# Encoder block on one core: the last stage's loads in program order on SP's queue at fixed steps, its first blocks fetched during the stage ahead, and its row sums one per step

## The chip, the core and the metric

The kernel runs on one core of a Trainium2 chip. The metric is the time of one execution in microseconds (us), taken on the device; lower is better. The profile is one further execution, recorded instruction by instruction. Engine names: PE is TensorE (matmul), PEld its weight loads, DVE is VectorE, ACT is ScalarE, POOL is GpSimd, SP is SyncE, which here only issues DMAs. Each engine works through its own list of instructions in order, and one that has to wait holds up those behind it on the same engine.

## The reference, cut to what matters

One encoder block on 1024 tokens of width 1024, in float32: a layer norm, one wide projection, dilated attention and a bidirectional recurrence, a merge with a second layer norm, then a gated feed-forward part with a third one. The change is in the feed-forward part:

```
gate, up = split(h @ w_ffn_in)                       # 1024 x 2816 each
h = layer_norm(ALPHA * h + (silu(gate) * up) @ w_ffn_out)   # w_ffn_out: 2816 x 1024
```

## The kernel before, in words

**Precision.** Every float32 operand is split into a high part `hi` (a cast, on ACT, line 204) and the rest `lo` (a subtraction, line 208, on POOL for weights, on DVE for activations here). `mm3` (lines 227 to 231) multiplies with three matmuls: hi by hi, one of hi and lo each way. Each writes one PSUM bank of 128x512.

**The two feed-forward stages.** `ffn_in` (line 1375) makes the 22 blocks of the activation, 128 rows by 1024 tokens each, and `ffn_out` (line 1480) multiplies them by `w_ffn_out`. Both use the seven products of a Strassen-Winograd scheme in place of eight. For `ffn_out` the activation is cut into a11, a12, a21, a22 (two halves of the 22 blocks, two halves of the tokens), the weights into b11, b12, b21, b22 (two halves of the rows, two halves of the columns). `combine` in `ffn_in` forms a11, a12, s2 (stored once, float32) and s1, s3, s4, a22 (stored already split, two tensors each) and writes them to scratch memory `gd` from SP's queue (lines 1408 and 1414). `ffn_in` ends with the last of its own seven products and `combine(10, 1)`.

**The work of `ffn_out`.** Six products run in the order 1, 2, 6, 5, 7, 3, each over 11 blocks j: 66 *steps*, numbered here from 0. A step multiplies one activation block by one weight block for four token tiles t: 12 matmuls, into four banks X (`pj`: products 1, 6, 7) or Z (`sd`: products 2, 5, 3). Product 4 follows, with the loops turned: for t = 0 to 3, 33 matmuls into X[t] over the a22 columns of that tile. After each of the six products its four banks are added to the halves of the row tiles Y[0] to Y[7] (`add`, line 1531: the "row sums", on DVE from PSUM). Product 4 gives the last sum of Y[4 + t].

**What a step needs.**

- the activation block: for products 1, 2, 6 a load `graw` (line 1504, three buffers), then `ghi` on ACT and `glo` on DVE (three buffers); for products 5, 7, 3 two loads straight into `ghi` and `glo` (line 1508);
- the weight block: 128x512 of `w_ffn_out` (`Wb11` and so on, line 1493; each has a buffer of its own), combined on DVE (`right`, lines 1511 to 1529: five subtractions or additions for each j), then split into `w_hi`, `w_lo` (four buffers).

Product 4 needs `a22h` and `a22l` of its tile (line 1597, 704 KB each, two buffers: tiles 2 and 3 reuse those of 0 and 1).

**The end.** `finish(t)` (line 1535) makes the layer norm of one row tile: two `bn_stats` and an aggregate on DVE, a power on POOL (line 198), the scaling on ACT (line 252), a product with the gain on POOL (line 1550), a sum on DVE (line 1551), and a store from SP's queue (line 1552). Tile 7 is done in halves, on DVE alone. The order in the code is t = 0 to 3 inside the loop over product 4's tiles, then 4 to 7.

**What sets the order.** The program is written in the order of the code, then a scheduler places each engine's instructions by its own estimate of when they can start; buffers add the waits. Instructions under `high_priority` (the row sums) are drawn forward. So SP's list of DMA issues need not follow the code.

Of the kernel before, what the change touches and what calls it, by code (L numbers as in the profile page):

```python
# [10 lines left out]
F32 = mybir.dt.float32  # L11
F32R = mybir.dt.float32r
# [7 lines left out]
D = 1024  # L20
T = 1024
KT = D // 128
HALF = 512
# [3 lines left out]
NJ = NF // 2  # L27
# [54 lines left out]
class Block:  # L82
# [1292 lines left out]
    def ffn_in(self):  # L1375

        nc = self.nc
        with ExitStack() as es:
# [99 lines left out]
    OUT_G = {1: "a11", 2: "a12", 6: "s2", 5: "s1", 7: "s3", 3: "s4"}  # L1478

    def ffn_out(self):  # L1480
# [3 lines left out]
        with ExitStack() as es:  # L1484
            wb = es.enter_context(self.pool("fow"))
            rp = es.enter_context(self.pool("for", "right"))
            W, Y = {}, {}
            halves = [slice(HALF * h, HALF * (h + 1)) for h in range(2)]

            def load(n, j):  # L1490
                W[n, j] = t = wb.tile([128, HALF], F32, name=f"W{n}", tag=f"{n}{j}", bufs=1)
                k, c = int(n[1]) - 1, int(n[2]) - 1
                nc.sync.dma_start(t, self.wfo[128 * (j + NJ * k):128 * (j + NJ * k + 1), HALF * c:HALF * (c + 1)])

            def rows(t):
                Y[t] = y = rp.tile([128, D], F32, name="y2", tag=f"y2{t}", bufs=1)
                nc.sync.dma_start(y, self.ahs_d[t])

            def acts(p, j):
                d = self.gd[self.OUT_G[p]][j]  # L1500
                z = [rp.tile([128, HALF], F32R, name=f"g{n}", tag=f"g{n}", bufs=3) for n in ("hi", "lo")]
                if len(d) == 1:
                    r = self.ws.tile([128, HALF], F32, name="graw", tag="wsum", bufs=3)
                    nc.sync.dma_start(r, d[0])
                    self.split(*z, r, eng_lo="dve")
                else:
                    for t, s in zip(z, d):
                        nc.sync.dma_start(t.bitcast(F32), s)
                return z

# [24 lines left out]
            def finish(t):  # L1535
                y = Y[t]
# [16 lines left out]

            for j in range(NJ):
                load("b11", j)
            X = [self.ps_pj(t) for t in range(4)]
            Z = [self.ps_sd() for t in range(4)]
            late = {}
            for p in self.OUT_ORDER:
                bank = X if p in (1, 6, 7) else Z  # L1560
                for j in range(NJ):
                    if p == 1:
                        load("b21", j)
                        if j in (3, 5, 7, 9):
                            rows((j - 3) // 2)
                    if p == 2:
                        load("b12", j)
                        if j >= NJ - 3:
                            load("b22", j - NJ + 3)
                    if p == 6 and j + 3 < NJ:  # L1570
                        load("b22", j + 3)
                    if p == 5 and j in (1, 3, 5, 7):
                        rows(4 + j // 2)
                    if p == 5 and j == 9:
                        g2, b2 = (rp.tile([128, D], F32, name=n) for n in ("g2", "b2"))
                        for t, v in zip((g2, b2), self.ln["2"]):
                            nc.scalar.dma_start(t, bass.AP(tensor=v.tensor, offset=v.offset, ap=[[0, 128], [1, D]]))
                    g = acts(p, j)
                    w = self.granules()
                    w = [z.rearrange("p k c -> p (k c)") for z in w]  # L1580
                    self.split(*w, right(p, j))
# [8 lines left out]
                for t in range(4):  # L1590
                    for i, h in {1: ((0, 0),), 2: ((0, 0),), 6: ((0, 1),), 5: ((1, 1),), 7: ((1, 1),), 3: ((0, 1),)}[p]:
                        add(4 * i + t, h, bank[t])
            a22 = []
            for t in range(4):
                a22.append([rp.tile([128, NJ, 128], F32R, name=f"a22{z}", tag=f"a22{z}", bufs=2) for z in "hl"])
                for z, d in zip(a22[t], self.gd["a22"]):
                    nc.sync.dma_start(z.bitcast(F32), d[:, :, 128 * t:128 * (t + 1)])  # L1597
            for t in range(4):
# [4 lines left out]
                finish(t)  # L1603
            for t in range(4, 8):
                finish(t)
# [38 lines left out]
```

## Time and profile before

| | |
|---|---|
| time, median of 3 runs | 2185.49 us (2185.03 to 2187.88) |
| the profiled execution's own time | 2187.32 us |
| its span in the profile, first to last instruction | 2185.5 us |
| PE busy in the span | 2037.5 us (93%) |
| DVE, ACT, POOL busy | 1380.8, 920.1, 1217.8 us |
| mean clock granted to PE | 0.979 of full |
| last matmul of `ffn_in` before the first of `ffn_out` | about 1920.5 us |
| PE's waits in `ffn_out`, up to 1986 us | 9.24, 1.87, 12.15 and 11.86 us |

In rows of the timeline the first number is the start in us from the span's beginning, the second the length; "x3" means that three like instructions are merged into a row; a bracket at the end says how long the engine sat idle before it and what it was released by. SPq rows are DMA issues. In the table by stretches (windows) the columns are the stretch, its length, busy time of PE, PEld, DVE, ACT, POOL with the number of instructions, the granted PE clock as a share of full, the busy share of the DMA engines and GB/s.

### The profile page before, as it was taken

The numbers are of one execution on the slowest core, as the hardware profiler recorded it, in microseconds if no ns is written. First come the engines' busy times: TensorE is split into PE (matmuls) and PEld (weight loads), VectorE is DVE, ScalarE is ACT, GpSimd is POOL, SyncE is SP. The second block draws the span as 40 slices with busy tenths as digits, with TensorE's granted clock in tenths as the row PEclk, the third lists the DMA queues.
The fourth block names the chain that finished last, engine by engine and source line by source line (L and its number), as shares of the span: only waits on it lengthen the run. The fifth ranks groups of instructions, "written<-read, shape, count | busy, mean of one in ns | idle before, by whom it ended". The sixth has DMA issues, their size and how long they took to land.

```text
span 2185.5 us, 31268 instructions
## 1 busy us (share of the span) xinstructions
PE 2037.5 (93%) x10941; PEld 1677.8 (77%) x10941; DVE 1380.8 (63%) x2165; ACT 920.1 (42%) x1870; POOL 1217.8 (56%) x960
## 2 busy tenths in 40 slices
PE   4799999999999999999999999998999999957997
PEld 3678887778877888778887788786888888846886
DVE  7667646875378845867455523258778878757426
ACT  6544455443554436344463421244434434323421
POOL 3566553566436664655545763444667777623545
PEclk9899999999999999999999999999999999988999
DMA  5343442435333352434436663335444445395454
GB/s 205 98 129 102 150 143 83 145 113 164 113 122 125 125 168 95 132 116 133 150 101 218 216 222 120 105 113 164 154 149 146 166 142 179 126 340 170 140 193 159
DMA packets 296447, 324.20 MB, mean 148 GB/s; under 512 B 15905, under 2 KB 212834, under 8 KB 296290
## 3 DMA queue, kind: packets, MB, share of 16 engines
q1 hardware_dynamic: 288544, 295.76, 42.1%
q10 hardware_dynamic: 7746, 26.45, 3.1%
q8 instruction: 86, 1.41, 0.3%
q14 instruction: 71, 0.58, 0.1%
HBM read 211.78 MB, written 110.36 MB: 147 GB/s over the span
## 4 chain that ended last, share of the span: by engine, by line
PE 59%; DVE 6%; POOL 4%; DMA 4%; issue 4%; ACT 1%; SPq 1%; DVEq 0%; POOLq 0%; ACTq 0%
PE pj L229 12%; PE pj L230 12%; PE pj L231 12%; PE sd L231 6%; PE sd L229 6%; PE sd L230 6%; POOL w_lo L208 2%; DMA Wb<-in_w_ffn_out_dram 1%; PE sd L1023 1%; DVE hR L984 1%; DVE hR L983 1%; DMA wa<-in_w_in_dram 1%; DMA graw<-ga11f 1%; DVE qd L938 0%; SPq L1597 0%
## 5 line engine op out<-in xcount | busy, mean ns | idle before, releaser
L208 POOL TENSOR_TENSOR w_lo<-wa,w_hi 128x512 fp32r<-128x512 f32 x276 | 387.0, 1410 | 273.6 <-ACT w_hi L204 265.7
L204 ACT CAST w_hi<-wa 128x512 fp32r<-128x512 f32 x276 | 170.0, 618 | 227.8 <-PE pj L230 164.4
L208 POOL TENSOR_TENSOR w_lo<-wsum,w_hi 128x512 fp32r<-128x512 f32 x88 | 135.7, 1553 | 78.3 <-ACT w_hi L204 40.9
L208 POOL TENSOR_TENSOR w_lo<-f_raw,w_hi 128x512 fp32r<-128x512 f32 x66 | 109.0, 1664 | 66.6 <-ACT w_hi L204 65.5
L208 POOL TENSOR_TENSOR w_lo<-Wb,w_hi 128x512 fp32r<-128x512 f32 x55 | 74.2, 1350 | 119.3 <-ACT w_hi L204 114.1
L229 PE MATMUL pj<-xt1hi,w_hi 128*128 128x512 f32 x268 | 109.2, 408 | 22.0 <-ACT xt1hi L204 15.7
L230 PE MATMUL pj<-xt1lo,w_hi 128*128 128x512 f32 x268 | 107.6, 402 | 4.5 <-DVE xt1lo L208 4.5
L231 PE MATMUL pj<-xb22hi,w_lo 128*128 128x512 f32 x268 | 105.1, 392 | 2.4 <-POOL w_lo L208 2.4
L231 PE MATMUL pj<-xt1hi,w_lo 128*128 128x512 f32 x268 | 106.8, 399 | 0.0
L229 PE MATMUL pj<-xb22hi,w_hi 128*128 128x512 f32 x268 | 105.7, 394 | 0.1
L463 POOL TENSOR_TENSOR wa<-wa,wa 128x512 f32<-128x512 f32 x46 | 64.5, 1403 | 73.5 <-DVE ws L462 65.5
L230 PE MATMUL pj<-xb22lo,w_hi 128*128 128x512 f32 x268 | 104.8, 391 | 0.0
L208 POOL TENSOR_TENSOR w_lo<-ws,w_hi 128x512 fp32r<-128x512 f32 x46 | 67.4, 1469 | 63.0 <-ACT w_hi L204 60.9
L229 PE MATMUL pj<-w_hi,ghi 128*128 128x512 f32 x132 | 55.1, 418 | 35.1 <-ACT ghi L204 35.1
L485 ACT COPY wkeep<-pj 128x512 f32<-128x512 f32 x138 | 80.3, 582 | 11.4 <-DVE evh L377 5.9
L229 PE MATMUL pj<-xb11hi,w_hi 128*128 128x512 f32 x188 | 77.5, 413 | 7.0 <-DVE wkeep L402 5.5
L204 ACT CAST w_hi<-wsum 128x512 fp32r<-128x512 f32 x88 | 54.6, 620 | 65.1 <-PE sd L230 61.7
L1393 ACT ACTIVATE fth<-fc 128x512 f32<-128x512 f32 x44 | 27.8, 632 | 122.3 <-DVE fc L1392 122.3
L229 PEld LDWEIGHTS pj<-xt1hi,w_hi 128*128 128x128 f32 x268 | 51.8, 194 | 35.8 <-ACT xt1hi L204 16.3
L388 DVE TENSOR_TENSOR evh<-wkeep,pj 128x512 f32<-128x512 f32 x48 | 32.7, 680 | 73.7 <-PE pj L231 53.7
L975 ACT ACTIVATE hS<-hR,dec 128x128 f32<-128x128 f32 x112 | 44.5, 402 | 80.9 <-DVE hR L984 57.6
L229 PE MATMUL pj<-xt4hi,w_hi 128*128 128x512 f32 x188 | 74.8, 398 | 3.6 <-DVE evh L377 3.6
(405 smaller groups left out, 6703.6 us busy)
## 6 DMA issues: line engine op xcount, KB each, us to landing
wa<-in_w_in_dram SPq DMA_DIRECT2D x184, 256.0 KB, 3.1
f_raw<-in_w_ffn_in_dram SPq DMA_DIRECT2D x44, 512.0 KB, 4.2
Wb<-in_w_ffn_out_dram SPq DMA_DIRECT2D x44, 256.0 KB, 5.4
tg<-evh SPq DMA_DIRECT2D x32, 256.0 KB, 3.0
tg<-tg SPq DMA_DIRECT2D x16, 512.0 KB, 3.9
y<-ahs SPq DMA_DIRECT2D x16, 512.0 KB, 6.1
ah<-xt ACTq DMA_DIRECT2D x8, 512.0 KB, 6.6
rec<-hg ACTq DMA_DIRECT2D x8, 512.0 KB, 4.0
```

The source lines that it names most:

```text
L204: nc.scalar.copy(hi, src)
L208: e.tensor_sub(lo, src, hi.bitcast(F32))
L229: nc.tensor.matmul(ps, whi, xhi, start=first, stop=False, **kw)
L230: nc.tensor.matmul(ps, whi, xlo, start=False, stop=False, **kw)
L231: nc.tensor.matmul(ps, wlo, xhi, start=False, stop=last, **kw)
L388: nc.vector.tensor_add(t, add, ps)
L463: nc.gpsimd.tensor_sub(a["a21"], a["a11"], a["a21"])
L485: nc.scalar.copy(t, ps)
L975: nc.scalar.activation(S[:, c, :], E, AF.Copy, scale=dec[:, 1, c:c + 1])
L983: nc.vector.scalar_tensor_tensor(En, E, dec[:, 1, c:c + 1], ps[:, jj, :], op0=OP.mult, op1=OP.add)
L984: nc.vector.tensor_scalar(En, En, dec[:, 0, c:c + 1], None, op0=OP.mult)
L1393: nc.scalar.activation(th[:, s], c[:, s], AF.Tanh, scale=0.5)
```

## The change: what it does

1. **Kept in order.** All loads of `ffn_out` go through `queued`, which issues them from SP's queue and has the scheduler keep them in the order in which the code gives them. The stores of the finished rows do not go through it. The two vectors of the layer norm, which ACT's queue loaded, come through it as well.
2. **Fixed steps.** A table (`bulk`) says at which step each load that is not the step's own activation block is issued, right behind that block: b11 from block 4 at steps 0 to 6, b21 at 7 + j, b12 at 16 + j, b22 at 17 + j, rows Y[0] to Y[3] at 11 to 14, Y[4] to Y[7] at 33, 35, 37, 39, the vectors at 46 and 48, a22 of tiles 0 and 1 at 55 to 61. The a22 loads of tiles 2 and 3 stand at the head of their own turn of the loop over product 4's tiles.
3. **First blocks ahead.** `out_begin`, called in `ffn_in` ahead of its last product, loads b11 blocks 0 to 3 into the buffers `w_raw` (idle by then) and the first three `graw`, and splits step 0.
4. **Row sums one per step.** The four sums of products 1, 6 and 7 are given one by one in the steps of the next product (from its fifth block on after product 1); those of 2, 5 and 3 still come together.
5. **Finishing.** Tile 4 + t is finished in turn t; turns 0 and 1 also finish tiles 0, 1 and 2, 3.

The diff, cut to its core:

```diff
+            self.out_begin()
             next(held, None)
             combine(NJ - 1, 1)
...
+    def queued(self, o, i):
+        return self.tc.keep_in_program_order(self.nc.sync.dma_start(o, i))
...
+    def out_begin(self):
+        self.W = W = {}
+        for i in range(2):
+            r = self.wraw.tile([128, D], F32, name="w_raw", tag="wraw", bufs=2)
+            for k in range(2):
+                W["b11", 2 * i + k] = self.out_block(r[:, HALF * k:HALF * (k + 1)], "b11", 2 * i + k)
+            if i == 0:
+                raw = self.out_raw(1, 0)
+                g, w = self.flat(), self.flat()
+                self.split(*w, W["b11", 0])
+                self.split(*g, raw, eng_lo="dve")
+        self.begun = {(1, 0): (g, w)}
+        self.raws = {(1, j): self.out_raw(1, j) for j in (1, 2)}
...
+            def last_acts(t, i):
+                if i == 0:
+                    a22.append([rp.tile([128, NJ, 128], F32R, name=f"a22{z}", tag=f"a22{z}", bufs=2) for z in "hl"])
+                self.queued(a22[t][i].bitcast(F32), self.gd["a22"][i][:, :, 128 * t:128 * (t + 1)])
...
+            for j in range(NJ):
+                at(7 + j, load, "b21", j)
+                at(16 + j, load, "b12", j)
+                at(17 + j, load, "b22", j)
+            for t in range(4):
+                at(11 + t, rows, t)
+                at(33 + 2 * t, rows, 4 + t)
...
+                    if adds and (p != 2 or j > 4):
+                        add(*adds.pop(0))
...
-            a22 = []
             for t in range(4):
-                a22.append([rp.tile([128, NJ, 128], F32R, name=f"a22{z}", tag=f"a22{z}", bufs=2) for z in "hl"])
-                for z, d in zip(a22[t], self.gd["a22"]):
-                    nc.sync.dma_start(z.bitcast(F32), d[:, :, 128 * t:128 * (t + 1)])
-            for t in range(4):
+                if t >= 2:
+                    for i in range(2):
+                        last_acts(t, i)
                 for j in range(NJ):
                     self.mm3(X[t], a22[t][0][:, j, :], a22[t][1][:, j, :], *late[j], False, j == NJ - 1,
                              skip_group_check=True)
                 add(4 + t, 0, X[t])
-                finish(t)
-            for t in range(4, 8):
-                finish(t)
+                if t < 2:
+                    finish(2 * t)
+                    finish(2 * t + 1)
+                finish(4 + t)
```

**Three places in the order of instructions.** Numbers behind names only tell buffers apart. First, SP's list before, where loads for product 1 (`graw` of a11, blocks 7 and 8) stand among the weights of the later products, the last rows (`y2`) and the a22 blocks; blocks 9 and 10 come behind all of these:

```order
L1504 DMA graw_17712<-ga11f7_209 128x512
L1493 DMA Wb22_18111<-in_w_ffn_out_dram 128x512
L1493 DMA Wb22_18138<-in_w_ffn_out_dram 128x512
L1493 DMA Wb22_18165<-in_w_ffn_out_dram 128x512
L1493 DMA Wb22_18192<-in_w_ffn_out_dram 128x512
L1493 DMA Wb22_18219<-in_w_ffn_out_dram 128x512
L1504 DMA graw_17736<-ga11f8_210 128x512
L1493 DMA Wb22_18246<-in_w_ffn_out_dram 128x512
L1493 DMA Wb22_18273<-in_w_ffn_out_dram 128x512
L1497 DMA y2_18400<-ahs4_119 128x1024
```

The same blocks of product 1 on SP's list with the change:

```order
L1484 DMA graw_17688<-ga11f7_209 128x512
L1484 DMA Wb21_17696<-in_w_ffn_out_dram 128x512
L1484 DMA graw_17712<-ga11f8_210 128x512
L1484 DMA Wb21_17720<-in_w_ffn_out_dram 128x512
L1484 DMA graw_17736<-ga11f9_211 128x512
L1484 DMA Wb21_17744<-in_w_ffn_out_dram 128x512
L1484 DMA graw_17760<-ga11f10_212 128x512
L1484 DMA Wb21_17768<-in_w_ffn_out_dram 128x512
L1484 DMA graw_17784<-ga12f0_213 128x512
```

One weight block now stands between two activation blocks; the rest of b21, b12, b22, the rows and a22 moved behind them.

Second, the end of SP's list before, from the last block of product 3 on (`y2_17608`, `17658`, `17708`, `17758` are Y[0] to Y[3], `y2_18400` is Y[4]):

```order
L1508 DMA glo_19112<-gs4l10_300 128x512
L1597 DMA a22h_19148<-ga22h_301 128x11x128
L1597 DMA a22l_19149<-ga22l_302 128x11x128
L1552 DMA out_0_dram<-y2_17608 128x1024
L1597 DMA a22h_19152<-ga22h_301 128x11x128
L1597 DMA a22l_19153<-ga22l_302 128x11x128
L1552 DMA out_0_dram<-y2_17658 128x1024
```

The same place with the change (`y2_17794`, `17820`, `17846`, `17872` are Y[0] to Y[3], `18382`, `18428`, `18474` are Y[4] to Y[6]):

```order
L1484 DMA glo_19118<-gs4l10_300 128x512
L1594 DMA out_0_dram<-y2_17794 128x1024
L1594 DMA out_0_dram<-y2_17820 128x1024
L1594 DMA out_0_dram<-y2_18382 128x1024
L1594 DMA out_0_dram<-y2_17846 128x1024
L1594 DMA out_0_dram<-y2_17872 128x1024
L1594 DMA out_0_dram<-y2_18428 128x1024
L1484 DMA a22h_19286<-ga22h_301 128x11x128
L1484 DMA a22l_19287<-ga22l_302 128x11x128
L1594 DMA out_0_dram<-y2_18474 128x1024
L1484 DMA a22h_19336<-ga22h_301 128x11x128
L1484 DMA a22l_19337<-ga22l_302 128x11x128
```

The a22 blocks of tile 2 moved from ahead of every store to behind six of them, the sixth that of Y[5]; those of tile 3 from behind Y[0]'s store to behind Y[6]'s.

Third, DVE's list between the `glo` of the first and of the second block of product 6. Before:

```order
L208 TENSOR_TENSOR glo_18087<-graw_18088,ghi_18086 128x512
L1520 TENSOR_TENSOR wt2_18202<-Wb22_18111,Wb11_17512 128x512
L208 TENSOR_TENSOR glo_18114<-graw_18115,ghi_18113 128x512
L1533 TENSOR_TENSOR y2_17608<-y2_17608,sd_17530 128x512
L1533 TENSOR_TENSOR y2_17658<-y2_17658,sd_17531 128x512
```

With the change:

```order
L208 TENSOR_TENSOR glo_18077<-graw_18078,ghi_18076 128x512
L1565 TENSOR_TENSOR Wb21_17844<-Wb21_17844,Wb11_17576 128x512
L1568 TENSOR_TENSOR Wb12_18091<-Wb22_18118,Wb12_18091 128x512
L1561 TENSOR_TENSOR Wb11_17600<-Wb12_18120,Wb11_17600 128x512
L1570 TENSOR_TENSOR Wb21_17818<-Wb21_17818,Wb22_18089 128x512
L1562 TENSOR_TENSOR wt2_18200<-Wb22_18056,Wb11_17532 128x512
L1561 TENSOR_TENSOR Wb11_17624<-Wb12_18149,Wb11_17624 128x512
L208 TENSOR_TENSOR glo_18106<-graw_18107,ghi_18105 128x512
```

One combination of weights stood between the two before, six do now: many of the combinations moved from ahead of product 2 into products 2 and 6.

More of the change, by code (lines that the diff above doesn't have):

```diff
@@ L1478, with flat, out_block, out_raw @@
     OUT_G = {1: "a11", 2: "a12", 6: "s2", 5: "s1", 7: "s3", 3: "s4"}
+    OUT_ROWS = {1: ((0, 0),), 2: ((0, 0),), 6: ((0, 1),), 5: ((1, 1),), 7: ((1, 1),), 3: ((0, 1),)}
+    def queued(self, o, i):
+        return self.tc.keep_in_program_order(self.nc.sync.dma_start(o, i))
+    def flat(self):
+        return [z.rearrange("p k c -> p (k c)") for z in self.granules()]
+    def out_block(self, t, n, j):
+        k, c = int(n[1]) - 1, int(n[2]) - 1
+        self.queued(t, self.wfo[128 * (j + NJ * k):128 * (j + NJ * k + 1), HALF * c:HALF * (c + 1)])
+        return t
+    def out_raw(self, p, j):
+        r = self.ws.tile([128, HALF], F32, name="graw", tag="wsum", bufs=3)
+        self.queued(r, self.gd[self.OUT_G[p]][j][0])
+        return r
+    def out_begin(self):
[11 more added lines that the diff above has]
+        self.raws = {(1, j): self.out_raw(1, j) for j in (1, 2)}
     def ffn_out(self):
@@ L1535, in finish @@
             def finish(t):
-                y = Y[t]
+                y, (g2, b2) = Y[t], gains
                 mv = self.stats(rp, y, "2")
@@ L1552, in finish, with at @@
                     nc.sync.dma_start(self.out[128 * t:128 * (t + 1), :], y)
-            for j in range(NJ):
-                load("b11", j)
+            bulk = {}
+            def at(step, f, *a):
+                bulk.setdefault(step, []).append((f, *a))
+            for j in range(4, NJ):
+                at(j - 4, load, "b11", j)
+            for j in range(NJ):
+                at(7 + j, load, "b21", j)
[5 more added lines that the diff above has]
+            for i in range(2):
+                at(46 + 2 * i, vector, i)
+                for t in range(2):
+                    at(55 + 4 * t + 2 * i, last_acts, t, i)
             X = [self.ps_pj(t) for t in range(4)]
             Z = [self.ps_sd() for t in range(4)]
-            late = {}
+            late, adds, step = {}, [], 0
             for p in self.OUT_ORDER:
@@ L1561, in ffn_out @@
                 for j in range(NJ):
[L1562 to L1581, printed above, removed]
+                    if (p, j) in self.begun:
+                        g, w = self.begun[p, j]
+                    else:
+                        g, w = acts(p, j), self.flat()
+                        self.split(*w, right(p, j))
+                    for f, *a in bulk.pop(step, []):
+                        f(*a)
                     if p == 3:
@@ L1589, in ffn_out @@
                                  skip_group_check=True)
-                for t in range(4):
-                    for i, h in {1: ((0, 0),), 2: ((0, 0),), 6: ((0, 1),), 5: ((1, 1),), 7: ((1, 1),), 3: ((0, 1),)}[p]:
-                        add(4 * i + t, h, bank[t])
-            a22 = []
+                    if adds and (p != 2 or j > 4):
+                        add(*adds.pop(0))
+                    step += 1
+                assert not adds
+                adds = [(4 * i + t, h, bank[t]) for t in range(4) for i, h in self.OUT_ROWS[p]]
+                if p in (2, 5, 3):
+                    while adds:
+                        add(*adds.pop(0))
             for t in range(4):
-                a22.append([rp.tile([128, NJ, 128], F32R, name=f"a22{z}", tag=f"a22{z}", bufs=2) for z in "hl"])
-                for z, d in zip(a22[t], self.gd["a22"]):
-                    nc.sync.dma_start(z.bitcast(F32), d[:, :, 128 * t:128 * (t + 1)])
-            for t in range(4):
+                if t >= 2:
+                    for i in range(2):
+                        last_acts(t, i)
                 for j in range(NJ):
```

19 lines of the change are left out of this document (10 added, 9 removed).

## The prediction

> **What bounds the kernel now.** I read the page first, then PE's stretches over the last stage, then PE's and SP's timelines there.
>
> ```profile
> span 2185.5 us, 31268 instructions
> 1920.00:1930.00 10.00, 0.76 (x4) 0.34 (x3) 3.00 (x6) 3.30 (x6) 2.69 (x3) 0.74 0.99 343
> 1950.00:1960.00 10.00, 0.96 (x5) 0.45 (x3) 6.66 (x10) 0.62 (x1) 1.57 (x2) 0.77 1.05 385
> 2000.00:2020.00 20.00, 20.00 (x89) 16.40 (x88) 19.97 (x21) 8.11 (x14) 11.85 (x8) 1.00 0.35 93
> ```
>
> After its span the execution has 2187.32 - 2185.5 = 1.8 us of its own, and it lies 1.8 us above the median of 2185.49; so a change of the span, added to the median, gives the time I forecast. From 2000 us on PE is full; ahead of that lie stretches in which it hardly works while the DMA engines are full (the last two columns). Its own timeline has the holes:
>
> ```profile
> 1917.49 0.50 PE L229 MATMUL sd<-xt4hi,w_hi 128*128 128x512 f32 x1 [0.78 <-DVE fu L1399]
> 1929.74 0.80 PE L229 MATMUL pj<-w_hi,ghi 128*128 128x512 f32 x1 [9.24 <-ACT ghi L204]
> 1935.00 0.40 PE L229 MATMUL pj<-w_hi,ghi 128*128 128x512 f32 x1
> 1942.48 0.50 PE L229 MATMUL pj<-w_hi,ghi 128*128 128x512 f32 x1 [1.87 <-ACT ghi L204]
> 1963.11 0.80 PE L229 MATMUL pj<-w_hi,ghi 128*128 128x512 f32 x1 [12.15 <-ACT ghi L204]
> 1969.18 0.40 PE L229 MATMUL pj<-w_hi,ghi 128*128 128x512 f32 x1
> 1986.23 0.80 PE L229 MATMUL pj<-w_hi,ghi 128*128 128x512 f32 x1 [11.86 <-ACT ghi L204]
> 1989.71 1.09 PE L231 MATMUL pj<-w_hi,glo 128*128 128x512 f32 x4
> ```
>
> Four waits, 35.1 us, all in product 1. SP says why: product 1's `graw` come after the a22 blocks.
>
> ```profile
> 1969.39 6.83 SPq L1597 DMA_DIRECT2D a22h<-ga22h  x1
> 1978.75 2.81 SPq L1504 DMA_DIRECT2D graw<-ga11f  x2
> 2048.11 0.32 SPq L1508 DMA_DIRECT2D ghi<-gs1h  x1
> 2050.83 0.32 SPq L1508 DMA_DIRECT2D ghi<-gs1h  x1
> ```
>
> The two last rows, one step apart in the full stage, give the step: 2.72 us, 0.227 a matmul. After each long wait PE is slow for a while: 12 matmuls from 1929.74 to 1935.00 take 5.26 us instead of 2.72, 14 from 1963.11 to 1969.18 take 6.07 instead of 3.18, 8 from 1986.23 to 1989.71 take 3.48 instead of 1.82. That is 2.5 + 2.9 + 1.7 = 7.1 us at half clock; after the wait of 1.87 us there is none.
>
> **The change part by part.**
>
> *Order kept in product 1: removes.* With one or two weight blocks between activation blocks the `graw` come three steps ahead, and all four holes go: 35.1 + 7.1 = **42.2 us** at most. No row speaks for more, as PE does the same matmuls.
>
> *First blocks ahead: adds a little back.* On SP they stand behind the store of s3's low part, and ACT and DVE meet them in the middle of `ffn_in`'s end:
>
> ```profile
> 1914.13 0.32 SPq L1414 DMA_DIRECT2D gs3l<-gl  x1
> wa<-in_w_in_dram SPq DMA_DIRECT2D x184, 256.0 KB, 3.1
> 1916.75 0.69 DVE L1399 TENSOR_TENSOR fu<-wkeep,sd 128x512 f32<-128x512 f32 x1 [0.64 <-PE sd L231]
> 1920.66 0.68 DVE L1400 SCALAR_TENSOR_TENSOR fc<-fth,sd 128x512 f32<-128x512 f32 x1
> 1922.14 0.62 ACT L204 CAST gh<-s 128x512 fp32r<-128x512 f32 x1 [2.56 <-DVE s L1430]
> ```
>
> The third of these loads, `graw` of block 0, is issued some 1.3 us after 1914.13 and lands 3.1 later at 1918.5; with ACT's cast of 0.62 PE starts step 0 at 1919.2, while its work ahead ends at 1916.7: a wait of 2.5 where 0.78 is now. Step 0 and the last product of `ffn_in`, 24 matmuls, end at 1924.7. Step 1 needs its `ghi`, which on ACT is queued behind the cast of s4 and so behind DVE's last `fc`, s4 and that cast: 1920.66 to 1922.76 is 2.1 us now, another 0.62 for `ghi` and the hand-overs make 2.9. I add 0.4 for step 3. Net: 2.5 - 0.8 + 2.9 + 0.4 = **5 us**. Bounds: 2 (a landing as fast as can be, step 1 hidden) to 9 (one more block late).
>
> *DVE in products 2 and 6: adds.* The 55 combinations of weights were half done during PE's holes. They now lie between the `glo`. From the first row sum of product 1, which has to wait for that product's end, to the last `glo` of product 6, DVE's list has 85 instructions: 55 combinations, 20 `glo`, 8 row sums, 2 `bn_stats`. What one costs, and what POOL's `w_lo` does to it:
>
> ```profile
> 1994.73 1.88 DVE L1533 TENSOR_TENSOR y<-y,pj 128x512 f32<-128x512 f32 x3
> 2007.64 0.69 DVE L1528 TENSOR_TENSOR Wb<-Wb,Wb 128x512 f32<-128x512 f32 x1
> 2008.25 1.78 DVE L208 TENSOR_TENSOR glo<-graw,ghi 128x512 fp32r<-128x512 f32 x1
> 2008.17 1.31 POOL L208 TENSOR_TENSOR w_lo<-Wb,w_hi 128x512 fp32r<-128x512 f32 x1 [1.11 <-ACT w_hi L204]
> ```
>
> They follow each other at 0.60 us; the one that meets a `w_lo` takes 1.78 instead of 0.69. There is one `w_lo` a step: 85 x 0.60 + 21 x 1.09 = 51 + 22.9 = 74 us, less some 3 for the ten that read PSUM or one tensor and are not stopped (the three row sums above ran at full pace beside a `w_lo`). PE's 21 steps last 57.1, and the matmuls with `glo` stand behind eight others of their step, 1.8 us. So 71 - 59 = 12 us are short, and about 3 more go at the start, where DVE waits for the first b12 block: **15 us**. Bounds: 0, since at 2000 to 2020 us PE stays full with DVE at 19.97 of 20 us, and 22, if nothing overlaps. I take 15, as DVE was full there with 21 instructions in 20 us and has to do 30 in that time now (85 in 57.1).
>
> The Trainium skill ("SBUF — State Buffer", SBUF: two separate sides) says that DVE instructions with two SBUF inputs and GpSimd's take a shared port pair for the whole instruction, and the other fully blocks. By its whole 1.3 us for each `w_lo` this term would be 4 us more.
>
> *Products 5, 7, 3: nothing.* Matmuls and loads are the same; two loads a step are issued two steps ahead (the rows at 2048.11 and 2050.83) and a row, vector or a22 block between them takes less than the 2 x 2.72 us of lead. If that cover fails, a block of 704 KB costs 1 or 2 us, once each.
>
> *The end of SP's list: adds most.* Before, the a22 blocks of tile 2 were issued when tile 0's matmuls let go of the buffer:
>
> ```profile
> 2150.79 0.53 SPq L1597 DMA_DIRECT2D a22h<-ga22h  x1
> 2151.38 0.81 SPq L1597 DMA_DIRECT2D a22l<-ga22l  x1
> 2157.46 0.34 SPq L1552 DMA_DIRECT2D out_dram<-y  x1
> 2158.92 0.19 PEld L231 LDWEIGHTS pj<-t4hi,a22l 128*128 128x128 f32 x1 [0.42 <-DMA a22l<-ga22l]
> ```
>
> From issue to the last byte 2158.9 - 2150.8 = 8.1 us, which tile 1's matmuls (7.5 us) just cover. Now six stores stand ahead of them; SP stops at each until its row is finished, and behind SP's wait stand the blocks for which PE waits. Rows for the finish:
>
> ```profile
> 2143.77 1.28 DVE L1533 TENSOR_TENSOR y<-y,sd 128x512 f32<-128x512 f32 x2 [28.80 <-PE sd L231]
> 2151.03 0.69 DVE L1533 TENSOR_TENSOR y<-y,pj 128x512 f32<-128x512 f32 x1 [0.64 <-PE pj L231]
> 2162.00 1.29 DVE L194 BATCH_NORM_STATS2 bn<-y 128x6 f32<-128x512 f32 x2
> 2161.41 1.25 ACT L252 ACTIVATE y<-y,mv 128x1024 f32<-128x1024 f32 x1 [1.49 <-DVE mv L251]
> 2148.33 0.55 POOL L198 TENSOR_TENSOR mv<-mv,mhalf 128x1 f32<-128x1 f32 x1 [12.25 <-DVE mv L197]
> 2151.57 4.77 POOL L1550 TENSOR_TENSOR y<-y,g 128x1024 f32<-128x1024 f32 x2 [0.66 <-ACT y L252]
> 2158.95 8.11 POOL L1550 TENSOR_TENSOR y<-y,g 128x1024 f32<-128x1024 f32 x3
> 2179.24 1.21 DVE L1551 TENSOR_TENSOR y<-y,b 128x1024 f32<-128x1024 f32 x1
> 2174.34 0.68 DVE L1533 TENSOR_TENSOR y<-y,pj 128x512 f32<-128x512 f32 x1
> 2180.38 1.40 DVE L1545 SCALAR_TENSOR_TENSOR y<-y,mv,b 128x512 f32<-128x512 f32 x2
> ```
>
> Let E be the first sum of product 3 (2143.77 now). With the change 16 matmuls of tile 0 are left at E instead of 32, so tile 1 ends at E + 49 x 0.227 = E + 11.1. DVE needs six instructions at 0.6, aggregates and hand-overs, POOL a power, ACT 1.25: POOL's first product with the gain starts at E + 6.3. From there on POOL's products (2.36 each) and DVE's sums (1.21) of Y[0], Y[1], Y[4], Y[2], Y[3], Y[5] take turns, as POOL's three at 2158.95 did, stretched from 7.1 to 8.1 us by DVE's between them; with five powers: 14.2 + 7.3 + 2.8 = 24.3. Y[5] is done at E + 30.6; its store and 1 us of issue, then 8.1: tile 2's a22 is there at E + 39.7, and PE has waited **28 us**. Tile 2's matmuls take 7.5, then Y[6] goes alone through sum, `bn_stats`, power, ACT, POOL, DVE: 0.7 + 1.3 + 0.4 + 0.6 + 0.3 + 1.25 + 2.4 + 1.2 + hand-overs = 8.4, and again 1 + 8.1: PE waits **17 us** for tile 3. Both are long waits, so half clock follows, 2.4 us each by the mean of the three above: **4.8 us**. Given back: Y[7] is then last alone, its sum to DVE's last row 4.3 us instead of 2181.78 - 2174.34 = 7.4: **3 us**. Sum: 28 + 17 + 4.8 - 3 = **47 us**. Bounds: 38, if POOL's and DVE's parts of two rows overlap and the blocks land in 5 us, and 52.
>
> The Trainium skill ("TensorE: Matmul & The Clock Gate", Part 1: The HAM clock gate) states half clock for a window of about 3.4 us after an idle window as long; that would make 1.7 instead of 2.4 for each wait. This trace's first two waits have more than that, its third agrees.
>
> *Row sums one per step, vectors on SP:* 0. The sums lie on DVE with the work counted above, the vectors have 18 steps until they are used; without that cover a row sum would cost 0.6.
>
> *Sum:* -42 + 5 + 15 + 47 = **+25 us**, 2185.5 + 25 = 2210.5 us.
>
> **The rivals.**
>
> *DVE keeps up (15%).* The combinations fit beside `glo` as they do at 2000 to 2020 us. For it: PE is full there. Against: the count of 85. Then -42 + 5 + 47 = +10: 2195.5.
>
> *SP is free for a22 in time (5%), and it comes out not slower.* The mechanism is SP's queue: if the six rows don't hold it, a22 of tile 2 is issued at E + 3.6, when tile 0's buffer is free, and lands as tile 1 ends; the 47 us go down to -3 and the time is 2185.5 - 42 + 20 - 3 = 2160.5. The point from which the change gains is an end below 42 - 20 = 22 us: Y[5] done some 25 us sooner than I have it, at about E + 6. For it: DVE's part of each row is short, and the DMA engines are idle by then. Against: SP waited for rows to be finished before, too:
>
> ```profile
> SPq L1552 <- DVE y L1551: 13.8, 3, 5.7
> ```
>
> Three stores held it for 13.8 us in all; what stood behind them then was only stores.
>
> *Product 1 still starves (10%).* Loads of up to 1 MB a step at 385 GB/s (1950 us) take all of the 2.72 us; if that leaves holes of two steps with half clock after, 10 us more: 2220.
>
> That the loads do not stand as said is no rival: the lists show them.
>
> **How the numbers follow.** The forecast has 70%, the rivals 15, 5 and 10. Predicted: 2210, the forecast's own sum. Its bounds with those of the unknown costs added in part (about 10 on either side), and the first and third rival, make 2195 to 2222. About 0.2%, 4.4 us, is what a measurement of this kernel can tell from no change. Faster by more: the second rival, 5%. Within: 4%, the first rival's part in which the end is at its lower bound of 38 too (-42 + 5 + 38 = +1). Slower: 91%.
>
> **What would show it.** Right: PE in product 1 without the waits of 9 to 12 us; DVE full in products 2 and 6 with PE waiting for `glo`; in product 4 two PE waits on `a22`, of 28 and 17 us, and SP waiting for DVE's sum of Y[5] just ahead. Wrong: tile 2's matmuls following tile 1's at once; or a PE wait for `glo` of under 5 us in all; or waits on `graw` in product 1.

## The result, and the profile after

The changed kernel takes 2209.74 us (median of 4 runs, 2206.67 to 2210.63) where the kernel before takes 2185.26 on the same chip: a ratio of 1.0108, 95% interval 1.009 to 1.0125. So it is 24.5 us slower. The profiled execution took 2210.36 us. Where a kernel's executions were disturbed, its ratio and interval below leave them out.

The first view is the page's head and PE's stretches (busy microseconds and instructions of PE, PEld, DVE, ACT and POOL, then granted clock, DMA share, GB/s).

```profile
span 2208.6 us, 31268 instructions
1950.00:1960.00 10.00, 10.00 (x46) 8.29 (x45) 4.56 (x7) 4.11 (x8) 4.99 (x4) 1.00 0.99 363
1980.00:1990.00 10.00, 3.08 (x8) 2.42 (x8) 9.80 (x13) 2.55 (x5) 10.00 (x3) 0.67 0.87 309
2000.00:2010.00 10.00, 6.16 (x23) 4.71 (x22) 10.00 (x15) 1.61 (x3) 3.12 (x2) 0.87 0.36 106
2030.00:2120.00 90.00, 90.00 (x398) 74.54 (x397) 16.05 (x25) 24.32 (x40) 43.07 (x33) 1.00 0.78 254
2140.00:2160.00 20.00, 0.34 (x2) 0.00 (x0) 15.17 (x17) 4.74 (x4) 13.60 (x8) 0.60 0.45 167
```

Before, PE was busy 0.76 us between 1950 and 1960 and full from 2000 on. Now it is full in product 1, has holes in products 2 and 6 in which DVE, and in one of them POOL, is full, is full again in products 5, 7 and 3, and stands still for 20 us at the end.

PE's own timeline of the changed kernel has these holes and what ended each:

```profile
1918.00 0.50 PE L229 MATMUL pj<-w_hi 128*128 128x512 f32 x1 [2.06 <-ACT w_hi L204]
1928.64 0.67 PE L229 MATMUL pj<-w_hi,ghi 128*128 128x512 f32 x1 [3.31 <-ACT ghi L204]
1987.00 0.79 PE L230 MATMUL sd<-w_lo,ghi 128*128 128x512 f32 x1 [6.92 <-POOL w_lo L208]
2007.89 2.08 PE L231 MATMUL pj<-w_hi,glo 128*128 128x512 f32 x4 [3.84 <-DVE glo L208]
2022.15 1.20 PE L231 MATMUL pj<-w_hi,glo 128*128 128x512 f32 x4 [1.62 <-DVE glo L208]
2026.25 1.19 PE L231 MATMUL pj<-w_hi,glo 128*128 128x512 f32 x4 [1.08 <-DVE glo L208]
2162.73 0.77 PE L229 MATMUL pj<-t4hi,a22h 128*128 128x512 f32 x1 [22.39 <-DMA a22h<-ga22h]
2165.04 0.80 PE L231 MATMUL pj<-t4hi,a22l 128*128 128x512 f32 x1 [1.11 <-DMA a22l<-ga22l]
2189.89 0.76 PE L229 MATMUL pj<-t4hi,a22h 128*128 128x512 f32 x1 [14.64 <-DMA a22h<-ga22h]
2192.18 0.79 PE L231 MATMUL pj<-t4hi,a22l 128*128 128x512 f32 x1 [1.09 <-DMA a22l<-ga22l]
```

The waits of 9 to 12 us on product 1's activations are gone. In their place stand 5.4 us at the stage's start, 13.5 us in products 2 and 6, and 39.2 us in product 4.

SP's list (its queue, SPq) shows why PE waits at the end, and DVE's list beside it what SP waits for. Of DVE the first two rows are the first sums of product 3 and the last step of the last three of those six rows; the others are the sums of Y[6] and Y[7].

```profile
2139.48 17.35 SPq L1594 DMA_DIRECT2D out_dram<-y  x6
2156.92 0.53 SPq L1484 DMA_DIRECT2D a22h<-ga22h  x1
2183.46 0.34 SPq L1594 DMA_DIRECT2D out_dram<-y  x1
2183.89 0.52 SPq L1484 DMA_DIRECT2D a22h<-ga22h  x1
```

```profile
2127.46 1.28 DVE L1575 TENSOR_TENSOR y<-y,sd 128x512 f32<-128x512 f32 x2 [30.02 <-PE sd L231]
2148.71 7.76 DVE L1593 TENSOR_TENSOR y<-y,gb 128x1024 f32<-128x1024 f32 x3
2175.29 0.69 DVE L1575 TENSOR_TENSOR y<-y,pj 128x512 f32<-128x512 f32 x1 [18.82 <-PE pj L231]
2200.87 0.69 DVE L1575 TENSOR_TENSOR y<-y,pj 128x512 f32<-128x512 f32 x1 [17.44 <-PE pj L231]
```

The sixth row is done at 2156.47, SP issues tile 2's blocks at 2156.92, and PE starts tile 2 at 2162.73; then the same once more with Y[6] alone.

Both sides of the account can now be read. I call E the first sum of product 3, as the prediction does, and count the stage from where PE begins its first wait in it: 1917.49 - 0.78 = 1916.7 before, 1918.00 - 2.06 = 1915.9 after. Up to E that is 227.1 us before and 211.5 after. Some matmuls of product 4 run ahead of E: PE's timelines show 9 before and 17 after, 8 more (1.8 us). On equal work the change gains 227.1 - (211.5 - 1.8) = **17.4 us** up to E. From E to the end it is 41.7 us before and 81.1 after, on equal work 82.9: it loses **41.2 us**. The difference, 23.8, less the 0.8 us by which the stage began earlier, is but for rounding the 23.1 us between the two spans.

### The profile page after: what moved, and what is told of

Same layout as the page of the kernel before. It is cut to its first block, busy times and chain, and to the rows that moved or that the text cites. A ratio compares the mean times of both kernels' runs of the same rounds, so it can differ in the third digit from the quotient of the medians.

```text
span 2208.6 us, 31268 instructions
## 1 busy us (share of the span) xinstructions
PE 2048.6 (93%) x10941; PEld 1685.4 (76%) x10941; DVE 1380.7 (63%) x2165; ACT 919.4 (42%) x1870; POOL 1234.5 (56%) x960
## 4 chain that ended last, share of the span: by engine, by line
PE 56%; DVE 8%; DMA 4%; issue 4%; POOL 4%; ACT 2%; SPq 0%; DVEq 0%; POOLq 0%; ACTq 0%
PE pj L229 12%; PE pj L231 12%; PE pj L230 12%; PE sd L231 5%; PE sd L229 5%; PE sd L230 5%; POOL w_lo L208 2%; PE sd L1023 1%; ACT p L801 1%; DMA a22l<-ga22l 1%; DVE p L823 1%; DVE y L1593 1%; DVE hR L984 1%; DMA wa<-in_w_in_dram 1%; DVE qd L938 1%
## 5 line engine op out<-in xcount | busy, mean ns | idle before, releaser
L208 POOL TENSOR_TENSOR w_lo<-wsum,w_hi 128x512 fp32r<-128x512 f32 x88 | 135.6, 1551 | 78.0 <-ACT w_hi L204 41.2
L229 PEld LDWEIGHTS pj<-xt1hi,w_hi 128*128 128x128 f32 x268 | 51.8, 194 | 37.1 <-ACT xt1hi L204 17.4
L231 PE MATMUL pj<-xt2hi,w_lo 128*128 128x512 f32 x188 | 74.7, 397 | 3.8 <-POOL w_lo L208 3.8
```

Of the source, the lines that this page charges most:

```text
L208: e.tensor_sub(lo, src, hi.bitcast(F32))
L229: nc.tensor.matmul(ps, whi, xhi, start=first, stop=False, **kw)
L231: nc.tensor.matmul(ps, wlo, xhi, start=False, stop=last, **kw)
```

## The experiments

My theory was: the end loses because SP, held at the stores of unfinished rows, holds back the blocks for which PE waits; the middle gives back part of the gain because DVE has more to do in products 2 and 6 than fits. The rivals were that the rows' finishing sets the end in any case, and that late transfers make the holes in the middle. Three further runs price the two remaining parts, the first blocks and the order kept.

| kernel | stage up to E | E to end | ratio to before, 95% interval |
|---|---|---|---|
| before | 227.1 | 41.7 | |
| changed | 211.5 | 81.1 | 1.0108, 1.009 to 1.0125 |
| a22 ahead of the stores | 211.2 | 41.3 | 0.9919, 0.9906 to 0.9932 |
| a22 behind three stores | 212.4 | 52.7 | 0.9987, 0.9975 to 0.9999 |
| before with the change's end | 227.7 | 83.3 | 1.0186, 1.0173 to 1.0199 |
| combinations in their step | 204.3 | 81.0 | 1.0069, 1.0057 to 1.0081 |
| `w_lo` on DVE | 206.0 | 81.5 | 1.0073, 1.006 to 1.0085 |
| both mended | 201.5 | 41.2 | 0.9873, 0.9856 to 0.989 |
| the same, `w_lo` on DVE | 196.1 | 41.2 | 0.9856, 0.9843 to 0.9869 |
| the same again | 195.2 | 41.2 | 0.9835, 0.9815 to 0.9855 |
| the same, first blocks late | 197.6 | 41.3 | 0.9871, 0.9852 to 0.989 |
| changed, first blocks late | 214.9 | 81.7 | 1.0116, 1.0103 to 1.0129 |
| before, order alone | 219.2 | 43.6 | 0.9969, 0.9957 to 0.9981 |

The two middle columns are worked out for each kernel as above, from its own trace. Behind E lie 122 matmuls in the changed kernel and in those made from it (125 with the combinations in their step), 130 before and with the change's end, and 135 with the order alone; one takes 0.23 us.

### a22 ahead of the stores

```diff
+            for t in (2, 3):
+                for i in range(2):
+                    last_acts(t, i)
             for t in range(4):
-                if t >= 2:
-                    for i in range(2):
-                        last_acts(t, i)
                 for j in range(NJ):
```

> The changed kernel, but the a22 blocks of tiles 2 and 3 stand on SP ahead of the finished rows' stores. My theory (SP, held by six stores, holds back the blocks for which PE waits): the two PE waits of 22.4 + 1.1 and 14.6 + 1.1 us go, and with them the half clock behind them. SP still has Y[0]'s store between the two tiles' blocks, which is free about when tile 1 ends, so a wait of up to 2 us may stay. What then ends last are the rows themselves on POOL and DVE: end at about E + 39 where it is E + 81 now, so 38 to 45 us less, 2165 to 2172 us. Rival (the rows' finishing on POOL and DVE sets the end and PE's waits only fill time that is there anyway): less than 10 us, 2200 us or more.

It took 2166.68 us, 43 less than the changed kernel. SP's list at the end:

```profile
2129.74 0.53 SPq L1484 DMA_DIRECT2D a22h<-ga22h  x1
2136.56 0.34 SPq L1594 DMA_DIRECT2D out_dram<-y  x1
2137.22 0.53 SPq L1484 DMA_DIRECT2D a22h<-ga22h  x1
2138.76 22.30 SPq L1594 DMA_DIRECT2D out_dram<-y  x6
```

The blocks are asked for at 2129.74 and 2137.22, SP is then held for 22.3 us all the same, but only stores stand behind it. Of PE's waits in product 4 one is left:

```profile
2146.59 0.50 PE L231 MATMUL pj<-t4hi,a22l 128*128 128x512 f32 x1 [1.25 <-DMA a22l<-ga22l]
```

The end shrinks from 81.1 to 41.3 us. The rival falls: the rows do set the end of this kernel, but 40 us sooner.

### a22 behind three stores

```diff
             for t in range(4):
-                if t >= 2:
-                    for i in range(2):
-                        last_acts(t, i)
...
                 finish(4 + t)
+                if t < 2:
+                    for i in range(2):
+                        last_acts(t + 2, i)
```

> The changed kernel, but the a22 blocks of tile 2 stand on SP behind three of the stores (Y[0], Y[1], Y[4]) and those of tile 3 behind the other three, each one turn earlier. If my theory (the wait is the time until the last row ahead on SP is finished, plus the load) holds in its amount too, it can be worked out from the changed kernel's trace: Y[4] is done at E + 19.0, a22h of tile 2 is there some 6 us after its issue, at about E + 25.4, where tile 1 ends at E + 12.9: one wait of 12 us, tile 2 ends 12.5 later at E + 38; tile 3's blocks, issued behind Y[5] at E + 29, are there before that, so no second long wait; tile 3 ends at E + 45.4 and the kernel 8 us later, at E + 54 instead of E + 81: 27 us less, 2179 to 2187 us. Rival (any stores ahead cost about the same, for instance since PE's clock or the load's own time makes most of it): two waits stay, not under 2200 us.

2181.95 us, from E to the end 52.7 where 54 was worked out. SP is held by three stores, and then by the other three:

```profile
2136.49 7.35 SPq L1594 DMA_DIRECT2D out_dram<-y  x3
2143.94 0.53 SPq L1484 DMA_DIRECT2D a22h<-ga22h  x1
2149.09 4.76 SPq L1594 DMA_DIRECT2D out_dram<-y  x3
2153.95 0.53 SPq L1484 DMA_DIRECT2D a22h<-ga22h  x1
```

PE has one long wait, for tile 2, and none for tile 3:

```profile
2149.67 0.77 PE L229 MATMUL pj<-t4hi,a22h 128*128 128x512 f32 x1 [12.31 <-DMA a22h<-ga22h]
```

So the price goes with the last row ahead of the blocks, as the theory has it, and not with there being stores ahead at all.

### The kernel before with the change's end

```diff
             for t in range(4):
-                a22.append([rp.tile([128, NJ, 128], F32R, name=f"a22{z}", tag=f"a22{z}", bufs=2) for z in "hl"])
-                for z, d in zip(a22[t], self.gd["a22"]):
-                    nc.sync.dma_start(z.bitcast(F32), d[:, :, 128 * t:128 * (t + 1)])
-            for t in range(4):
+                if t >= 2:
+                    last_acts(t, True)
...
                 add(4 + t, 0, X[t])
-                finish(t)
-            for t in range(4, 8):
-                finish(t)
+                if t < 2:
+                    finish(2 * t)
+                    finish(2 * t + 1)
+                finish(4 + t)
```

(`last_acts(t, True)` loads a tile's two blocks, kept in program order on SP; those of tiles 0 and 1 stay where they were.)

> The kernel before with only the end of the change: rows finished in turn with tiles 0 and 1, a22 of tiles 2 and 3 queued on SP behind the six stores. My theory: the end alone does the loss. Six rows are done some 30 us after the first sum of product 3, then 6 to 8 us until tile 2's blocks are there; with 16 matmuls more behind that sum than in the changed kernel the wait is shorter by 2 or 3 us; 36 to 42 us slower than before, 2221 to 2228 us. Rival (the loss needs the rest of the change, the order kept on the queue or the earlier end of the products): less than 10 us, 2195 us or less.

2225.18 us where before took 2185.41, 39.8 more. PE's two waits are there again, in a kernel that has nothing else of the change:

```profile
2175.30 0.76 PE L229 MATMUL pj<-t4hi,a22h 128*128 128x512 f32 x1 [21.75 <-DMA a22h<-ga22h]
2201.72 0.77 PE L229 MATMUL pj<-t4hi,a22h 128*128 128x512 f32 x1 [14.27 <-DMA a22h<-ga22h]
```

The end alone makes the loss: on the same work as before, the stretch from E to the end is 41.6 us longer, and the stage up to E is as long as before.

### The combinations of products 5, 7 and 3 in their own step

```diff
                 if p == 5:
-                    nc.vector.tensor_add(b21, b21, b11)
+                    self.tc.keep_in_program_order(nc.vector.tensor_add(b21, b21, b11))
...
-                    nc.vector.tensor_sub(b12, b22, b12)
+                    self.tc.keep_in_program_order(nc.vector.tensor_sub(b12, b22, b12))
...
-                nc.vector.tensor_sub(b21, b21, b22)
+                self.tc.keep_in_program_order(nc.vector.tensor_sub(b21, b21, b22))
```

> The changed kernel, but the 33 weight combinations of products 5, 7 and 3 are kept in program order on DVE, so that they lie in those products instead of 2 and 6. My theory (DVE has more to do in products 2 and 6 than fits): 33 x 0.60 = 20 us leave DVE there, which is more than is short; PE's waits for glo and w_lo in these products (13.5 us, and about 3 at half clock) go, 12 to 18 us less than the changed kernel, 2192 to 2198 us. Rival (the holes come from weight blocks that land late, DVE's full row is only what it does meanwhile): the holes stay, within 4 us of 2209.7.

2201.56 us, 8 less than the changed kernel: the sign is the theory's, the size is not. The holes of 6.92 and 3.84 us are gone though the loads are the same, and in the changed kernel DVE waits only 0.2 us for a block between 1965 and 2025: blocks that land late did not make them. What is left in products 2 and 6 is 1.43 and 1.79 us, and product 7 has a new wait. The row is PE's, and those behind it DVE's just ahead of it:

```profile
2055.97 1.21 PE L229 MATMUL pj<-w_hi,ghi 128*128 128x512 f32 x4 [2.77 <-ACT w_hi L204]
```

```profile
2052.10 2.48 DVE L1575 TENSOR_TENSOR y<-y,sd 128x512 f32<-128x512 f32 x4 [17.90 <-PE sd L231]
2054.50 12.15 DVE L1568 TENSOR_TENSOR Wb<-Wb,Wb 128x512 f32<-128x512 f32 x11
```

Kept behind all that DVE was given before them, product 7's combinations stood behind the row sums of product 5, which wait for that product's last matmul; its first step had no weight in time. I had not counted on this wait.

### `w_lo` of products 2 and 6 on DVE

```diff
-                        self.split(*w, right(p, j))
+                        self.split(*w, right(p, j), eng_lo="dve" if p in (2, 6) else "pool")
```

> The changed kernel, but the low parts of the weights of products 2 and 6 are made on DVE and not on POOL, all else equal. It tells two forms of the DVE reason apart. If what costs is that DVE and POOL stop one another (1.09 us on DVE for each of 22 w_lo, and a POOL that waits 10 us for one w_lo), DVE gets 22 x 0.60 = 13 us of new work and loses 24 of stretch: the wait for w_lo of 6.9 us goes and 6 to 12 us are gained, 2198 to 2204 us. If what costs is DVE's number of instructions alone, 107 x 0.60 = 64 us in products of 57 give new holes, 5 to 15 us slower, 2215 to 2225 us.

2200.59 us, 9 less, though DVE has 22 instructions more in products it already filled. The groups by line, of the changed kernel and then of this one, over 1965 to 2025 us (count, busy and mean ns of one):

```profile
L1568 DVE TENSOR_TENSOR Wb<-Wb,Wb 128x512 f32<-128x512 f32 x11 | 10.7, 977 | 0.0
L1562 DVE TENSOR_TENSOR wt<-Wb,Wb 128x512 f32<-128x512 f32 x7 | 6.9, 989 | 1.2 <-POOL w_lo L208 1.2
L208 POOL TENSOR_TENSOR w_lo<-wt,w_hi 128x512 fp32r<-128x512 f32 x10 | 21.1, 2125 | 11.8 <-ACT w_hi L204 11.8
L208 POOL TENSOR_TENSOR w_lo<-Wb,w_hi 128x512 fp32r<-128x512 f32 x6 | 18.1, 3033 | 9.2 <-ACT w_hi L204 9.2
```

```profile
L1568 DVE TENSOR_TENSOR Wb<-Wb,Wb 128x512 f32<-128x512 f32 x11 | 7.7, 696 | 0.0
L208 DVE TENSOR_TENSOR w_lo<-wt,w_hi 128x512 fp32r<-128x512 f32 x11 | 7.6, 705 | 0.0
L1562 DVE TENSOR_TENSOR wt<-Wb,Wb 128x512 f32<-128x512 f32 x7 | 4.8, 707 | 0.0
```

With POOL out of the way these two groups of DVE's combinations take 0.70 us instead of 0.98, and a low part costs 0.7 us of one engine where it cost POOL 2.1 to 3.0. So the two engines stopping one another is a large part of the term, and the mere number of instructions is not all of it; two holes are left, 3.65 us for `glo` and 3.00 for DVE's `w_lo`. DVE shows no idle time in the 10 us ahead of either, so I put them down to its own amount of work.

The Trainium skill ("SBUF — State Buffer", SBUF: two separate sides) has it that one of the two holds a shared port pair for a whole instruction and the other fully blocks; these rows agree in that each is faster without the other.

### Both mended

The a22 blocks ahead of the stores as above, and the combinations kept in order, but each asked for four steps ahead of its use:

```diff
+                    for q in order[step + 4:step + 5]:
+                        if q[0] in (5, 7, 3):
+                            early[q] = right(*q)
```

The step itself then takes `early.pop((p, j), None) or right(p, j)`.

> The a22 blocks ahead of the stores as in the first of these kernels, and the combinations of products 5, 7 and 3 kept in program order on DVE, but each four steps ahead of its use and not in the step itself. My theory: in the kernel with the combinations in their own step, 7 us of the 17 that DVE costs went and 10 stayed, of which about 5 were new (a wait of 2.8 + 0.4 us and half clock in product 7, where the first step's combination stood behind the row sums); four steps of lead take these too. From 2166.7: 10 to 13 us less, 2152 to 2158 us. Rival (the place of the combinations is not what keeps the rest): 7 us less as before, 2159 to 2161 us, and a wait for the weights at the start of product 7 that stays.

The ratio of 0.9873 to before's 2184.62 makes 2156.9 us (from two executions): 10 less than with the a22 blocks alone, the theory's figure. The intervals of the two ratios are too wide to tell 10 from the rival's 7; the trace does, as the wait for weights at the start of product 7 is gone. PE has no wait in products 5, 7 and 3; in products 2 and 6 there are five for `glo`, of 3.9 us in all, the longest 1.81.

> As the kernel with both mended, and the low parts of the weights of products 2 and 6 on DVE. My theory: with 52 instructions left there DVE has room for 22 more (74 x 0.60 = 44 us of 57), and POOL's lock is gone; the last waits for glo in these products (1.4 + 1.8 us and their half clock) go: 2 to 5 us less than the kernel with both mended. Rival (with DVE no longer full the lock costs nothing, and what waits for glo is left is DVE's order): no difference, within 2 us, or some us more since w_lo now stands behind row sums in DVE's list.

(The edit on top is the one line that puts `w_lo` on DVE.) 2153.17 us, 3.7 less, within what was expected; the two intervals overlap, but in the trace the stage up to E is 5.4 us shorter. PE has two waits left in products 2 and 6, of 0.29 and 1.62 us.

This kernel beats both: it is 1.4% faster than before, and by the two ratios (0.9856 / 1.0108) 2.5% faster than the changed one.

### The first blocks asked for late

```diff
-            self.out_begin()
             next(held, None)
             combine(NJ - 1, 1)
+            self.out_begin()
```

> The changed kernel, but the first blocks of the last stage are asked for after the last stores of the stage ahead, not during it. My theory: the three waits that part costs are less than what it saves. The loads start after the last store, about 1925, land 3 us later, and step 0 starts at about 1930; PE waits 10 to 11 us in one piece where 2.1 + 3.3 and their half clock are now: 3 to 9 us slower than the changed kernel, 2213 to 2219 us. Rival (the early casts on ACT and DVE hold up the end of the stage ahead by more than the head start is worth): 2 to 6 us faster, 2204 to 2208 us.

2210.03 us; neither theory's figure, since the time cannot be told from the changed kernel's. In the trace the stage up to E is 3.4 us longer. SP's list, of the changed kernel and of this one, shows what the head start costs: the last store of the stage ahead is issued 12.9 us after PE's first wait (at 1915.9) there, and 6.8 us after it (at 1910.2) here.

```profile
1928.82 0.32 SPq L1414 DMA_DIRECT2D gs4l<-gl  x1
```

```profile
1917.04 0.32 SPq L1414 DMA_DIRECT2D gs4l<-gl  x1
1917.41 0.94 SPq L1484 DMA_DIRECT2D w_raw<-in_w_ffn_out_dram  x2
```

PE then has one wait for its first blocks, of 9.01 us, in place of two:

```profile
1923.04 0.79 PE L229 MATMUL pj<-w_hi 128*128 128x512 f32 x1 [9.01 <-ACT w_hi L204]
```

To tell the small difference apart, I made the same edit in the last kernel of the section before and ran it beside that kernel.

> The kernel with the a22 blocks first, the combinations four steps ahead and the low parts of the weights of products 2 and 6 on DVE once more, as the partner of the next one: 2151 to 2156 us.

> That kernel with the first blocks asked for after the stage ahead. In the changed kernel that made the last stage 3.4 us longer in the trace (one wait of 9.0 + 0.8 for two of 2.1 + 3.3), but not the time, which spreads by 4 us. My theory: the head start is worth about a step, 2.7 us, and the holes of products 2 and 6 hid part of it; here 2 to 6 us slower than its partner. Rival (it is worth nothing: DVE, held by POOL's low parts during the head start, finishes the stage ahead 6 us later, and all that is won is lost again): within 1.5 us of its partner.

By their ratios the partner took 2148.6 us and this kernel 2156.5. The time says 8 us, but the same partner had 2153.17 in the section before, and the stage up to E is only 1.9 us longer than the mean of the partner's two traces; the rest is time spent ahead of the stage, where the two kernels do the same. So the head start is worth something, 2 to 3 us by the traces. How much of the rest is chance stays open.

### The order alone

```diff
-                nc.sync.dma_start(y, self.ahs_d[t])
+                self.tc.keep_in_program_order(nc.sync.dma_start(y, self.ahs_d[t]))
```

and the same for every other load of `ffn_out` on SP, in the kernel before.

> The kernel before with only the order of its own list kept: every load of the last stage on SP in program order, all at the places the kernel before gives them, a22 of all four tiles ahead of the stores, nothing fetched during the stage ahead. My theory, as a sum: the later three waits of product 1 and their half clock go (1.9 + 12.2 + 11.9 + 4.6 = 30.5 us); step 0 cannot start before its blocks are there, behind the last store, eleven b11 blocks, one b21 block and its own activation block, about 1936, so that 9 us come on top of the first wait; and DVE is short in products 2 and 6, 15 us. Net 6 us less than before, with these terms' ranges 2172 to 2186 us. Rival (the gain in product 1 needs the fixed steps and the early blocks): not under 2190 us. If DVE is not short here: 2164 us.

2178.8 us, 5.8 less than before, and 6 were worked out. PE's longest waits in the stage:

```profile
1935.92 0.80 PE L229 MATMUL pj<-w_hi,ghi 128*128 128x512 f32 x1 [19.10 <-ACT ghi L204]
2019.20 2.07 PE L231 MATMUL pj<-w_hi,glo 128*128 128x512 f32 x4 [4.55 <-DVE glo L208]
```

One wait until everything ahead of the first activation block has come, none in the rest of product 1, and DVE short again in products 2 and 6: keeping the order does what it was counted for in product 1 without the fixed steps, and the hole in DVE comes with it.

## Why the prediction was right, point by point

The sum met the result, 25 against 24.5 us, better than its terms did: 3 too little for the first blocks, 2 too little for DVE and 6 too much for the end nearly cancel. That much of the match is luck; the mechanisms below are not.

**Order kept in product 1, -42.** Right. None of the four waits is left. That the whole 42.2 us were gained follows from the account: up to E 17.4 were gained in all, so 24.8 came in their place. The new holes hold 18.0 us (2.06 + 3.31 + 6.92 + 3.84 + 1.62 + 1.08 less the old 0.78), and the matmuls behind the first four, with a granted clock of 0.50 to 0.65, lose 1.7 + 1.7 + 1.6 + 1.4 = 6.4; 0.4 is left over.

**First blocks ahead, +5.** Right in kind, 3 us too small: waits of 2.06 and 3.31 us where 2.5 and 2.9 stood in the sum, 4.6 net of the old 0.78, but the half clock behind both, 3.4 us, was not in the sum. That makes 8.0, within the bounds of 2 to 9. Its price was counted against the kernel before, where the scheduler had fetched such blocks early too; what the head start saves against having none is 2 to 3 us by the traces.

**DVE in products 2 and 6, +15.** Right in size, and the mechanism half right. PE's waits there are 13.5 us, and some 3 of half clock come with them: about 17. The prediction let DVE pay 1.09 us for each `w_lo` and PE wait for `glo`. PE did wait 6.5 us for `glo`, but the longest wait, 6.92 us, was for a `w_lo` that POOL could not get done. POOL's row and the ends of DVE's stretch beside it:

```profile
1976.77 13.56 POOL L208 TENSOR_TENSOR w_lo<-Wb,w_hi 128x512 fp32r<-128x512 f32 x3 [3.53 <-ACT w_hi L204]
```

```profile
1977.32 0.68 DVE L1561 TENSOR_TENSOR w_raw<-Wb,w_raw 128x512 f32<-128x512 f32 x1
1985.15 0.68 DVE L1570 TENSOR_TENSOR Wb<-Wb,Wb 128x512 f32<-128x512 f32 x1
1986.03 1.47 DVE L1561 TENSOR_TENSOR Wb<-Wb,Wb 128x512 f32<-128x512 f32 x1 [0.20 <-DMA Wb<-in_w_ffn_out_dram]
```

For 8 us DVE's instructions follow each other at 0.60, none stretched; POOL, ready since 1976.77, comes through when DVE waits 0.20 us for a block. A DVE without gaps does not always shut POOL out. The `w_lo` just before this one came in behind one DVE instruction, and DVE's next, with no idle time ahead of it, was stretched, as the prediction had it:

```profile
1971.45 1.79 POOL L208 TENSOR_TENSOR w_lo<-Wb,w_hi 128x512 fp32r<-128x512 f32 x1 [2.92 <-ACT w_hi L204]
1972.01 1.78 DVE L1568 TENSOR_TENSOR Wb<-Wb,Wb 128x512 f32<-128x512 f32 x1
```

So the step that failed is who pays: the sum let DVE pay each time, and here POOL paid, and PE with it. What decides between the two stays open. Together with the first blocks, 20 were predicted and 25 measured.

**Products 5, 7, 3, nothing.** Right: PE is busy 90.00 of 90 us from 2030 on.

**The end, +47.** Right in mechanism, 6 us too large. The waits are 22.39 + 1.11 = 23.5 us where 28 stood, and 14.64 + 1.09 = 15.7 for 17. The first is shorter for four reasons. Tile 1 ended at E + 12.9 and not E + 11.1, since seven matmuls of product 3 run behind E as well, which the sum left out: 1.8 us. Y[5] was done at E + 29.0 and not 30.6: 1.6. SP issued the blocks 0.5 us after that and not 1: 0.5. And PE resumes when the high half is there, 5.8 us after its issue, and works 1.2 us before it waits for the low half; the sum let it stand until both are there, 8.1 us after the issue, which is when they came: 1.2. (Together 5.1; the sum's own E + 39.7 less E + 11.1 is 28.6.) Half clock cost 5.9 us where 4.8 stood: the first to the last matmul of tiles 2 and 3 are 12.1 and 10.6 us apart, full pace is 7.3, and the waits for the low half are 1.1 each. At the very end 3.5 us came back, 3 in the sum: Y[7]'s sum to the end of the span is 7.7 us instead of 11.2. These make 41.6, against the 41.2 of the account.

Two readings of the trace before were off here, without changing the sum. At E 24 matmuls of tile 0 were left before, not 32. And not only stores stood behind held stores there: behind Y[0]'s, issued at 2157.46, came the a22 blocks of tile 3. It cost nothing, as they went out at 2158.27, just as tile 1's matmuls ended.

**Row sums one per step and the vectors, 0.** Nothing was run on either, so their price stays open.

**The rivals.** "DVE keeps up" falls with the holes in products 2 and 6, "product 1 still starves" with the full stretches there. "SP is free for a22 in time" did not happen, and the first experiment made it happen: 2166.7 us, where the rival had 2160.5. On equal work 17.7 us were gained up to E where the rival counted 22, and the end was 1.4 us longer than before where it counted 3 shorter; the stage began 3.3 us sooner in that trace.

## What to carry to other kernels

A queue that keeps program order is as late as the slowest thing in it: before pinning loads on it, list the stores that stand ahead of each load and ask when their data is finished. Put what feeds the busiest engine ahead of what merely leaves. When a wait goes, the work that it was hiding has to fit somewhere: count the instructions of the other engines in the stretch that gets shorter, and keep early-ready work near its use, but a few steps ahead and not behind something that waits.

## What the runs showed of the hardware that was not expected

DVE instructions at 0.60 us each left POOL's `w_lo` no way in for 8 to 9 us, until DVE had a gap of 0.20 us. Others came in between DVE instructions without a gap, and DVE's next then took up to 1.78 us; what makes the difference the runs do not show. The same low part costs 1.3 us on POOL beside a DVE with gaps, 2.1 to 3.0 in the mean beside a full one, and 0.70 on DVE.

The granted clock was 0.50 from 2162.73 to 2171.2, 8.5 us, behind the wait of 22.39 us, and for 5.3 us behind that of 14.64, each with a wait of 1.1 us inside it. Before the change it was 0.50 for 5.7 us from 1963.11 on, behind a wait of 12.15 us and with none inside. The Trainium skill ("TensorE: Matmul & The Clock Gate", Part 1: The HAM clock gate) has about 3.4 us; here the measurement decides, and it is longer.

The time that a kernel takes up to this stage spreads by several us between executions: PE's first wait in the stage began at 1907.6 in one trace of the fastest kernel and at 1914.9 in another. What makes it was not looked into.
